# The gate table built 16 tokens at a time: two runs of half-precision matmuls back to back

## The chip, the cores and the metric

The kernel runs on one core of one Trainium2 chip. The metric is the device time of one execution in microseconds (us); lower is better. TensorE multiplies (its rows in the profile are PE for a matmul and PEld for the load of a matmul's weights, the stationary operand), VectorE (DVE) and ScalarE (ACT) do elementwise work, and transfers from memory are issued from the SP queue.

## The reference

One decoder layer on 256 tokens of width 1024: attention and pooling, an output projection, and then the part that matters here, a feed-forward layer (PEER) with 16,384 = 128 x 128 experts of one neuron each. Every token has 8 heads; each head picks 16 experts by two sub-keys of 128 entries, with softmax gates.

```python
def chunk(xc):
    q = jnp.einsum('cd,de->ce', xc, w_q)...reshape(C, PEER_HEADS, 2, half)
    s = jnp.einsum('chpk,pnk->chpn', q, sub_keys)
    sv, si = lax.top_k(s, K)
    ...
    eid = jnp.take_along_axis(cand_id, top_pos, axis=-1)      # 8 x 16 experts of a token
    gate = jax.nn.softmax(top_v, axis=-1)
    act = jax.nn.gelu(jnp.einsum('cd,chkd->chk', xc, expert_u[eid]))
    y = jnp.einsum('chk,chkd->cd', gate * act, expert_v[eid])
```

## The kernel before

The kernel does not gather experts. It computes S = U h for all 16,384 experts and all tokens, applies the gelu to get A, builds a dense gate table W (expert by token, nearly all zeros), and multiplies: G = W * A, then y = G V. There are three stages: a prefix (attention and projections, to about 131 us), phase 1 (the loop at L887: 16 steps of queries, then 128 steps of S, to 566 us) and phase 2 (the loop at L986, y = G V, to the end).

A step of phase 1 handles one tile of 128 rows of weights. `split` (L510) cuts the loaded tile into a high part on ScalarE (L501) and a low part on VectorE (L506), one step ahead of its use; `mm3` (L546) then issues 24 matmuls of 256 columns in a reduced float32 format, 16 from the high part (L551 and L552 in turn) and 8 from the low part (L555). Queries go into PSUM banks 1 to 3, S into banks 6 and 7.

Around these steps the program's order is written by the Python code itself: `after(d, f)` puts a function behind the matmuls of the step d steps later (`run_hooks`), and `run_bg` takes pieces of background work from a list, as many as a budget allows for each step.

The gate table is such background work. For each group of 8 tokens (`c8` from 0 to 31) `wtok` makes four half-precision tiles on VectorE in four pieces: two one-hot tables (`ohb`, `oha`) and `oha` times the high and the low half of the gate (`ah`, `al`). One step later (two for `c8` = 0) `wmm` (L778) issues 16 matmuls of 128 columns, two for each token, into two PSUM banks: 0 and 1 where `c8` is even, 2 and 3 where it is odd. A step after that `wput` (L793) takes the result out of PSUM: multiplied into A by VectorE (L798) where A is there already, copied by ScalarE (L801) elsewhere. `gelu` (L804) treats the tokens whose W is there and those whose W is not there apart; `have["W"]` holds how many there are.

In this text a run is an unbroken row of half-precision matmuls (L782 and L783 in turn), and a stretch is what stands between two runs: one, two or three steps of `mm3`.

Of the kernel before, what the change touches and what calls it, by code (L numbers as in the profile page):

```python
# [18 lines left out]
T = 256  # L19
D = 1024  # L20
# [39 lines left out]
class Loads:  # L60
    """DMAs in the order of their use; each is issued as soon as its pool has a free slot."""

# [25 lines left out]
def _body(ctx, tc, xT, c, w_ada, cols, w_in, pool_w, w_out, peer_wq, subkeys, peer_u, peer_v, final_g,  # L88
# [38 lines left out]

# [1 line left out]
    silc = prep.tile([P, D + 1], F32, name="silc")  # L129
# [51 lines left out]

# [1 line left out]
    nc.vector.memset(ones, 1.0)  # L183
    nc.vector.memset(silc[:, D:D + 1], 1.0)
    # per-head negated score bias of 128 queries and the 256 keys up to the last of them: ALiBi, the window
    # mask and the log of the number of branches; s of the first queries takes the rest of each row
    def score_bias(hs):
# [24 lines left out]
    def rsqrt(r, m, std):  # L212
        """r = 1/sqrt(m), one Newton step on the root of ScalarE."""
        nc.scalar.activation(std, m, AF.Sqrt)
        nc.vector.reciprocal(r, std)
        nc.vector.scalar_tensor_tensor(std, m, -0.5, r, op0=ALU.mult, op1=ALU.mult)
        nc.vector.tensor_mul(std, std, r)
        nc.vector.scalar_tensor_tensor(r, std, 1.5, r, op0=ALU.add, op1=ALU.mult)

    def rstd_rows(ps, psb):  # L220
        """psb[any partition, token] = 1/sqrt(sum/D + eps)."""
        m = prep.tile([P, 6], F32, name="m", bufs=2)
        nc.vector.tensor_scalar(m[:, 0:2], ps, 1.0 / D, EPS, op0=ALU.mult, op1=ALU.add)
        rsqrt(m[:, 2:4], m[:, 0:2], m[:, 4:6])
        dg = prep.tile([P, 2, P], F32, name="dg", bufs=1)
        for tb in range(2):
            nc.vector.tensor_scalar(dg[:, tb, :], ident, m[:, 2 + tb:3 + tb], None, op0=ALU.mult)
        nc.tensor.matmul(psb, lhsT=ones, rhs=dg.rearrange("p a t -> p (a t)"), start=True, stop=True)
# [6 lines left out]
    def keep_warm(n):  # L235
        """matmuls on ones while there is nothing to multiply: TensorE's clock is halved when it is idle"""
        for _ in range(n):
            nc.tensor.matmul(banks[5][:, 0, 0:P], lhsT=ones, rhs=ones, start=True, stop=True)
# [37 lines left out]

# [1 line left out]
    for k in range(KD):  # L278
# [29 lines left out]
        def mm(m, n):  # L308
            """product n (hi hi, hi lo, lo hi) of output block m: 0-7 q k, 8-11 u, 12-13 v"""
            if m < 12:  # L310
                wh, wl = (w0h, w0l) if m < 8 else (w1h, w1l)
                cs = slice(m * P, (m + 1) * P) if m < 8 else slice(512 + (m - 8) * P, 512 + (m - 7) * P)
                a, b = ((wh, hh), (wh, hl), (wl, hh))[n]
                nc.tensor.matmul(banks[m // 2][:, m % 2, :], lhsT=a[:, cs], rhs=b,
                                 start=(st and n == 0 and m % 2 == 0), stop=(sp and n == 2), skip_group_check=True)
            else:
                tb = m - 12
                a, b = ((hh, w1h), (hl, w1h), (hh, w1l))[n]
                nc.tensor.matmul(banks[6 + tb].rearrange("p a t -> p (a t)"), lhsT=a[:, tb * P:(tb + 1) * P],
                                 rhs=b[:, 0:512], start=(st and n == 0), stop=(sp and n == 2))  # L320
# [23 lines left out]

# [1 line left out]
    pra.close()  # L346
# [41 lines left out]
    def s2d(p):  # L388
        for h in (2 * p, 2 * p + 1):
            s = biast[:, h, :]  # L390
            mx = prep.tile([P, 6], F32, name="mx", bufs=4)
            # s = -score, mx = -max score
            for tb, cs, bs in ((0, slice(0, P), slice(256, 384)), (1, slice(P, 384), slice(P, 384))):
                nc.vector.tensor_tensor_reduce(
                    out=s[:, cs], in0=s[:, bs], in1=H[h]["ps"][:, cs], scale=1.0, scalar=-NEG,
                    op0=ALU.add, op1=ALU.min, accum_out=mx[:, tb:tb + 1])
            H[h]["s"], H[h]["mx"] = s, mx
# [92 lines left out]

# [1 line left out]
    x2 = xt  # L492
# [20 lines left out]

    # x2 in token rows, for the last residual
    turned = [banks[i].rearrange("p a t -> p (a t)") for i in (4, 5, 6, 0)]
# [30 lines left out]
    def mm3(o, n, ks=range(KD)):  # L546
        """o[128, T] += (tile n of 8 blocks [d, 128])^T h2"""
        hi, lo = splits[n]
# [8 lines left out]

    # queries: the first two tiles follow the arrival of h2
    # from here on: queries in banks 1 to 3, scores in 4 and 5, S in 6 and 7, W and y in 0 to 3
    def q_bank(n):  # L560
# [35 lines left out]

# [1 line left out]
    NA = 96  # L598
# [31 lines left out]
    def top16(sets):  # L630
        """the 16 largest and their places, for several (vals, idx, src) side by side"""
        lo, hi = slice(0, 8), slice(8, 16)
# [11 lines left out]
    def retrieval(tb):  # L644
# [7 lines left out]
        def second(hh):  # L652
            # pairs (a, b) of the sorted halves: a < 4 with all b, a >= 4 with b < 4; for any other pair
            # 16 pairs of these stand before it
            if hh == 0:
# [15 lines left out]
        def gates():  # L671
            g = S["gate"] = tk.tile([P, NH, TOPK], F32, name="gate")
            nc.vector.tensor_sub(g, S["tv"], S["tv"][:, :, 0:1].to_broadcast([P, NH, TOPK]))
            nc.scalar.activation(g, g, AF.Exp)
            # the places of the first choice, each twice, by half
            S["si2"] = tk.tile([P, 2, NH * TOPK, 2], F16, name="si2")
# [13 lines left out]
        def places():  # L690
            """(a, b) of a place: a = max(pos / 16, pos / 4 - 12), b = pos - min(16 a, 4 a + 48)"""
            sh = [P, NH * TOPK]
# [60 lines left out]

    WS = {}

    def wtok(c8, part):
# [7 lines left out]
        if part == 0:  # L764
            WS["b"] = wp.tile(sh, F16, name="ohb")
            nc.vector.tensor_tensor(out=WS["b"], in0=io, in1=pair(jT), op=ALU.is_equal)
        elif part == 1:
            WS["a"] = wp.tile(sh, F16, name="oha", bufs=1)
            nc.vector.tensor_tensor(out=WS["a"], in0=io, in1=pair(iT), op=ALU.is_equal)
        elif part == 2:  # L770
            WS["h"] = wp.tile(sh, F16, name="ah")
            nc.vector.tensor_tensor(out=WS["h"], in0=WS["a"], in1=pair(gh), op=ALU.mult)
        else:
            WS["l"] = wp.tile(sh, F16, name="al")
            nc.vector.tensor_tensor(out=WS["l"], in0=WS["a"], in1=pair(gl), op=ALU.mult)
            after(1 if c8 else 2, wmm, c8, WS["b"], WS["h"], WS["l"])

# [8 lines left out]
    def parts(lo, hi):  # L786
        """tiles lo..hi of the table, as slices of the two buffers that hold it"""
        for buf, at_, n in ((a0, 0, NA), (P2.get("a1"), NA, NK - NA)):
# [4 lines left out]
    def wput(c8, o):  # L793
        """W of 8 tokens: times A where A is there already, else left in its place"""
        ts = slice(c8 * 8, c8 * 8 + 8)
# [4 lines left out]
        for a, r in parts(have["A"], NK):  # L800
            nc.scalar.activation(a[:, :, ts], oT[:, r, :], AF.Copy, scale=1.0 / GSC)  # L801
        have["W"] = c8 * 8 + 8

    def gelu(i, bank):  # L804
        """A of tiles i, i + 1, times W for the tokens whose W is there"""
        (a, _), = parts(i, i + 2)
# [59 lines left out]

# [1 line left out]
    G = {}  # L868
# [44 lines left out]

# [1 line left out]
    step_no[0] = NQ + NK  # L915
# [62 lines left out]

    # the last tiles serve the first 128 tokens before the others, so that these can be finished early
    spare = [[p3.tile([P, D], F32R, name=x) for x in ("vh", "vl")] for _ in range(2)]  # L980
    spare.append([G[0][j].rearrange("p i t -> p (i t)") for j in (1, 2)])
    # in them, the last quarter of the columns of the other tokens goes to a bank of its own
    pieces = [slice(0, 512), slice(512, 768), slice(768, 1024)]
# [21 lines left out]

# [1 line left out]
    zs = [f3[:, (1 + tb) * D:(2 + tb) * D] for tb in range(2)]  # L1007
# [11 lines left out]
    def z_piece(tb, j, cs, y=None, x=None):  # L1019
        """z = y g2 + x2 and its sum of squares"""  # L1020
        z_add(tb, cs, ycols(tb, cs) if y is None else y, x2nat[:, tb, cs] if x is None else x)
        nc.scalar.activation(sqz[:, cs], zs[tb][:, cs], AF.Square, accum_out=scol(tb, j))
# [11 lines left out]
    def half_inv(tb, j, part):  # L1034
        """1 / (s + m / s): half of 1/sqrt(m), from s near sqrt(m)"""
        if part == 0:
# [98 lines left out]
```

## Time and profile before

| what | value |
|---|---|
| time, median of 3 executions | 928.67 us (928.41 to 928.76) |
| profiled execution, first to last instruction | 930.6 us |
| TensorE busy | 910.1 us, 98% of the span |
| VectorE busy | 691.6 us, 74% |
| ScalarE busy | 455.3 us, 49% |
| half-precision matmuls (L782, L783) | 512, from 306.5 to 540.6 us |

The profiled execution is told by its span alone; it is 1.9 us above the median of the three timed ones. A busy TensorE is one that has a matmul in flight: matmuls overlap, so the record of one (281 ns for 256 columns) is longer than the distance to the next. How fast they follow each other is read from their start times, or from how many of them a stretch holds.

### The profile page before, as it was taken

What the parts mean: (1) busy time and instruction counts of PE and PEld (TensorE: products, weight loads), DVE (VectorE), ACT (ScalarE), POOL (GpSimd) and SP (SyncE); (2) the same over time, 40 slices, a digit from 0 to 9 for tenths busy, and PEclk for the clock granted to TensorE, in tenths of its full rate; (3) what the DMA queues carried; (4) which work ended last, traced back from release to release, by engine and by line L of the source; (5) the groups of instructions that cost most, each with busy time, mean ns of one, the idle gap of its engine ahead of it and who ended that gap; (6) DMA issues with size and microseconds to landing.
All of it is one profiled execution on the core that took longest, in us unless ns stands there. A gap on an engine that the chain in (4) does not pass through costs nothing.

```text
span 930.6 us, 15919 instructions
## 1 busy us (share of the span) xinstructions
PE 910.1 (98%) x6283; PEld 830.6 (89%) x6283; DVE 691.6 (74%) x1285; ACT 455.3 (49%) x655; POOL 10.3 (1%) x19
## 2 busy tenths in 40 slices
PE   7999989999999999999999999999999999999996
PEld 7987889999999999999999998888878788888885
DVE  5999869898989778888888966555556656656665
ACT  3447355545555455454444445444446545444442
POOL 0000000000000000000000000000000000000001
PEclk7999989999999999999999999999999999999999
DMA  9987735455656555555555556666767766667551
GB/s 343 408 312 264 293 107 167 159 182 183 183 190 192 161 164 168 169 161 171 168 160 166 174 167 191 189 195 195 217 217 226 238 226 214 213 210 218 183 180 46
DMA packets 52061, 185.40 MB, mean 199 GB/s; under 512 B 6033, under 2 KB 6545, under 8 KB 51986
## 3 DMA queue, kind: packets, MB, share of 16 engines
q1 hardware_dynamic: 50402, 179.12, 59.4%
q0 software_dynamic: 1440, 5.25, 1.9%
q8 instruction: 49, 0.80, 0.4%
q14 instruction: 26, 0.21, 0.1%
q10 hardware_dynamic: 144, 0.01, 0.0%
HBM read 183.31 MB, written 1.05 MB: 198 GB/s over the span
## 4 chain that ended last, share of the span: by engine, by line
PE 87%; DVE 5%; DMA 4%; ACT 2%; issue 1%; SPq 0%; ACTq 0%; DVEq 0%
PE psum L976 33%; PE psum L551 14%; PE psum L552 14%; PE psum L555 14%; PE psum L441 3%; DMA raw<-in_peer_v_dram 3%; PE psum L782 2%; PE psum L783 2%; PE psum L568 1%; DVE junk L198 1%; DVE wlo L300 1%; PE psum L832 1%; DMA big<-in_w_in_dram 1%; ACT hi L501 1%; DVE lo L506 1%
## 5 line engine op out<-in xcount | busy, mean ns | idle before, releaser
L506 DVE TENSOR_TENSOR lo<-raw,hi 128x1024 fp32r<-128x1024 f32 x269 | 328.6, 1223 | 205.9 <-ACT hi L501 204.9
L501 ACT ACTIVATE hi<-raw 128x1024 fp32r<-128x1024 f32 x269 | 285.0, 1060 | 318.0 <-PE psum L976 153.7
L551 PE MATMUL psum<-h2h,hi 128*128 128x256 f32 x1128 | 273.4, 283 | 0.4 <-ACT q L823 0.4
L552 PE MATMUL psum<-h2l,hi 128*128 128x256 f32 x1128 | 269.7, 280 | 0.0
L551 PEld LDWEIGHTS psum<-h2h,hi 128*128 128x128 f32 x1128 | 213.1, 189 | 0.6 <-ACT q L823 0.6
L552 PEld LDWEIGHTS psum<-h2l,hi 128*128 128x128 f32 x1128 | 213.0, 189 | 0.0
L555 PE MATMUL psum<-h2h,lo 128*128 128x256 f32 x1128 | 154.5, 280 | 0.0
L555 PEld LDWEIGHTS psum<-h2h,lo 128*128 128x128 f32 x1128 | 141.7, 189 | 0.0
L976 PE MATMUL psum<-hi,h2h 128*128 128x512 f32 x486 | 132.8, 393 | 2.3 <-ACT hi L501 2.3
L976 PE MATMUL psum<-lo,h2h 128*128 128x512 f32 x486 | 131.4, 390 | 0.0
L976 PE MATMUL psum<-hi,h2l 128*128 128x512 f32 x486 | 131.3, 390 | 0.0
L976 PEld LDWEIGHTS psum<-hi,h2h 128*128 128x128 f32 x486 | 90.5, 188 | 22.5 <-ACT hi L501 3.5
L976 PEld LDWEIGHTS psum<-lo,h2h 128*128 128x128 f32 x486 | 91.3, 188 | 20.0
L976 PEld LDWEIGHTS psum<-hi,h2l 128*128 128x128 f32 x486 | 91.3, 188 | 19.8
L198 DVE SCALAR_TENSOR_TENSOR junk<-ada,silc 128x1025 f32<-128x1025 f32 x40 | 48.9, 1222 | 0.3
L801 ACT ACTIVATE a<-psum 128x256 f32<-128x256 f32 (+22 forms) x54 | 16.7, 352 | 60.8 <-DVE a L798 52.6
L883 DVE TENSOR_TENSOR h2l<-a,h2h 128x1024 fp32r<-128x1024 f32 x31 | 37.8, 1219 | 0.0
L782 PE MATMUL psum<-ah,ohb 128*128 128x128 f16 x256 | 33.1, 220 | 0.0
L783 PE MATMUL psum<-al,ohb 128*128 128x128 f16 x256 | 32.7, 218 | 0.0
L879 ACT ACTIVATE h2h<-a 128x1024 fp32r<-128x1024 f32 x31 | 32.4, 1045 | 0.0
L441 PE MATMUL psum<-cat,big 128*128 128x256 f32 x128 | 28.9, 382 | 0.0
L441 PEld LDWEIGHTS psum<-cat,big 128*128 128x128 f32 x128 | 23.9, 190 | 3.9 <-issue 0.8
(226 smaller groups left out, 807.9 us busy)
## 6 DMA issues: line engine op xcount, KB each, us to landing
raw<-in_peer_u_dram SPq DMA_DIRECT2D x128, 512.0 KB, 3.6
raw<-in_peer_v_dram SPq DMA_DIRECT2D x128, 512.0 KB, 4.3
ada<-in_w_ada_dram SPq DMA_DIRECT2D x40, 512.5 KB, 7.1
big<-in_w_in_dram SPq DMA_DIRECT2D x16, 512.0 KB, 9.2
raw<-in_peer_wq_dram SPq DMA_DIRECT2D x16, 512.0 KB, 3.7
a<-in_w_ada_dram POOLq DMA_DIRECT2D x8, 512.5 KB, 5.3
big<-in_w_out_dram SPq DMA_DIRECT2D x8, 512.0 KB, 6.5
out_dram<-a SPq DMA_DIRECT2D x4, 256.0 KB, 2.3
```

The source lines that it names most:

```text
L198: nc.vector.scalar_tensor_tensor(jk, blk, 1.0, sil, op0=ALU.mult, op1=ALU.mult, accum_out=ada[:, v * 8 + k:v * 8 + k + 1])
L441: nc.tensor.matmul(ob[m // 2][:, m % 2, :], lhsT=w[:, m * P:(m + 1) * P], rhs=cat[:, k, :], start=(n == 0 and m % 2 == 0), stop=(n == 7), ...
L501: nc.scalar.activation(hi, raw, AF.Copy)
L506: nc.vector.tensor_sub(lo, raw, hi.bitcast(F32))
L551: nc.tensor.matmul(o, lhsT=hi[:, cs], rhs=h2h[:, k, :], start=(k == 0), stop=False, skip_group_check=True)
L552: nc.tensor.matmul(o, lhsT=hi[:, cs], rhs=h2l[:, k, :], start=False, stop=False, skip_group_check=True)
L555: nc.tensor.matmul(o, lhsT=lo[:, cs], rhs=h2h[:, k, :], start=False, stop=(k == KD - 1), skip_group_check=True)
L782: nc.tensor.matmul(o[:, t, :], lhsT=b[:, pr, :, e], rhs=ah[:, pr, :, e], start=True, stop=False)
L783: nc.tensor.matmul(o[:, t, :], lhsT=b[:, pr, :, e], rhs=al[:, pr, :, e], start=False, stop=True)
L879: nc.scalar.activation(hi, a, AF.Copy)
L883: nc.vector.tensor_sub(lo, a, hi.bitcast(F32))
L976: nc.tensor.matmul(ycols(tb, cs) if o is None else o, lhsT=a[:, i % 4, tb * P:(tb + 1) * P], rhs=b[:, cs], start=st, stop=sp, skip_group_c ...
```

## The change

The runs of two neighbouring groups are issued together. `wtok` puts a finished group on a list, and only an odd group asks for the matmuls, one step later; `wmm2` then takes the groups from the end of the list, so that the odd one (banks 2 and 3) goes first and the even one (banks 0 and 1) directly behind it. `al` is written over `oha`, and the tiles have three buffers each. The two `wput` of a pair follow in one step, and `have["W"]` grows by 16.

```diff
+    WP = []
...
         if part == 0:
-            WS["b"] = wp.tile(sh, F16, name="ohb")
+            WS["b"] = wp.tile(sh, F16, name="ohb", bufs=3)
...
-            WS["a"] = wp.tile(sh, F16, name="oha", bufs=1)
+            WS["a"] = wp.tile(sh, F16, name="oha", bufs=3)
...
-            WS["h"] = wp.tile(sh, F16, name="ah")
+            WS["h"] = wp.tile(sh, F16, name="ah", bufs=3)
...
         else:
-            WS["l"] = wp.tile(sh, F16, name="al")
-            nc.vector.tensor_tensor(out=WS["l"], in0=WS["a"], in1=pair(gl), op=ALU.mult)
-            after(1 if c8 else 2, wmm, c8, WS["b"], WS["h"], WS["l"])
+            nc.vector.tensor_tensor(out=WS["a"], in0=WS["a"], in1=pair(gl), op=ALU.mult)
+            WP.append((c8, WS["b"], WS["h"], WS["a"]))
+            if c8 % 2:
+                after(1, wmm2)
+
+    def wmm2():
+
+        while WP:
+            wmm(*WP.pop())
...
-        have["W"] = c8 * 8 + 8
+        have["W"] = max(have["W"], c8 * 8 + 8)
```

On TensorE, the end of the first run before (numbers behind a name are buffers; `ohb` are the weights):

```order
L782 LDWEIGHTS ohb_3451
L782 MATMUL psum_137<-ah_3455,ohb_3451 128x128
L783 LDWEIGHTS ohb_3451
L783 MATMUL psum_137<-al_3499,ohb_3451 128x128
L551 MATMUL psum_137<-h2h_71,hi_3536 128x256
L552 MATMUL psum_137<-h2l_72,hi_3536 128x256
L551 MATMUL psum_137<-h2h_71,hi_3536 128x256
```

And the middle of the first run of the changed kernel (L789 and L790 are the L782 and L783 of before):

```order
L789 LDWEIGHTS ohb_3531
L789 MATMUL psum_137<-ah_3565,ohb_3531 128x128
L790 LDWEIGHTS ohb_3531
L790 MATMUL psum_137<-oha_3533,ohb_3531 128x128
L789 LDWEIGHTS ohb_3451
L789 MATMUL psum_137<-ah_3455,ohb_3451 128x128
L790 LDWEIGHTS ohb_3451
L790 MATMUL psum_137<-oha_3453,ohb_3451 128x128
```

Where a step of `mm3` followed the 16th half-precision matmul, 16 more of the next group follow it, without a wait in between; the run stands where the odd group's stood, behind the same step, and the place of the even group is empty.

On VectorE, the pieces behind the first two groups before:

```order
L775 TENSOR_TENSOR al<-oha,gl 128x1024
L506 TENSOR_TENSOR lo<-raw,hi 128x1024
L798 SCALAR_TENSOR_TENSOR a_1267<-psum,a_1267 128x46x8
L766 TENSOR_TENSOR ohb<-ion,jT 128x1024
L506 TENSOR_TENSOR lo<-raw,hi 128x1024
L798 SCALAR_TENSOR_TENSOR a_1267<-psum,a_1267 128x46x8
L769 TENSOR_TENSOR oha<-ion,iT 128x1024
```

And now:

```order
L775 TENSOR_TENSOR oha<-oha,gl 128x1024
L506 TENSOR_TENSOR lo<-raw,hi 128x1024
L767 TENSOR_TENSOR ohb<-ion,jT 128x1024
L506 TENSOR_TENSOR lo<-raw,hi 128x1024
L805 SCALAR_TENSOR_TENSOR a_1267<-psum,a_1267 128x46x8 x2
L770 TENSOR_TENSOR oha<-ion,iT 128x1024
```

The first of the two results taken out of PSUM has moved behind one more `lo`, to stand beside the second; everything else keeps its order.

## Rows read from the trace of the kernel before

**Rows 1.** The page: busy time of engines, and the granted TensorE clock in 40 slices.

```profile
PE 910.1 (98%) x6283; PEld 830.6 (89%) x6283; DVE 691.6 (74%) x1285; ACT 455.3 (49%) x655; POOL 10.3 (1%) x19
...
PEclk7999989999999999999999999999999999999999
```

**Rows 2.** Stretch of the table: length, busy PE, PEld, DVE, ACT, POOL; clock.

```profile
400.00:450.00 50.00, 50.00 (x480) 49.77 (x480) 42.34 (x56) 24.39 (x45) 0.00 (x0) 1.00 0.51 165
```

**Rows 3.** Timeline around one run: start us, length us, engine, line.

```profile
356.50 0.28 PE L551 MATMUL psum<-h2h,hi 128*128 128x256 f32 x1
356.51 0.19 PEld L552 LDWEIGHTS psum<-h2l,hi 128*128 128x128 f32 x1
356.62 0.28 PE L552 MATMUL psum<-h2l,hi 128*128 128x256 f32 x1
...
357.87 0.23 PE L782 MATMUL psum<-ah,ohb 128*128 128x128 f16 x1
...
357.94 0.22 PE L783 MATMUL psum<-al,ohb 128*128 128x128 f16 x1
...
358.74 0.22 PE L783 MATMUL psum<-al,ohb 128*128 128x128 f16 x1
...
358.77 0.36 PE L551 MATMUL psum<-h2h,hi 128*128 128x256 f32 x1
```

**Rows 4.** Stretches behind even groups: window, length, L552 matmuls (8 a step).

```profile
307.44:310.25 2.81, 1.87 (x8) 1.00 0.67 182
320.62:326.16 5.54, 3.73 (x16) 1.00 0.52 158
...
349.61:357.87 8.26, 5.59 (x24) 1.00 0.55 164
...
sum 102.18, PE 68.99; mean PE 4.31
```

**Rows 5.** Stretches behind odd groups, the same columns.

```profile
311.15:319.72 8.57, 5.79 (x24) 1.00 0.43 130
...
342.97:348.71 5.74, 3.86 (x16) 1.00 0.48 152
...
sum 106.01, PE 71.42; mean PE 4.46
```

**Rows 6.** Stretches of `mm3` away from runs, and the last one behind a run.

```profile
543.54:566.16 22.62, 15.44 (x64) 1.00 0.56 177
187.15:252.16 65.01, 44.37 (x184) 1.00 0.61 187
540.63:543.54 2.91, 1.93 (x8) 1.00 0.67 225
```

**Rows 7.** L552 from 131.5 to 306.5 us: duration in ns, minimum/median/maximum.

```profile
L552 PE MATMUL psum<-h2l,hi x472: 281/281/281, 132.1 to 305.5; 128*128 128x256 f32 x158
```

**Rows 8.** L552 in the stretch from 349.61 us, behind an even group.

```profile
L552 PE MATMUL psum<-h2l,hi x24: 276/276/281, 349.8 to 356.8; 128*128 128x256 f32 x24
```

**Rows 9.** L552 in the stretch from 358.77 us, behind an odd group.

```profile
L552 PE MATMUL psum<-h2l,hi x16: 281/281/281, 359.0 to 363.4; 128*128 128x256 f32 x16
```

**Rows 10.** Waits from 306 to 545 us: total us, times, longest.

```profile
ACT hi L501 <- PE psum L552: 39.0, 25, 1.8
DVE lo L506 <- ACT hi L501: 37.0, 56, 1.5
```

**Rows 11.** VectorE's timeline where its pieces are longest.

```profile
489.12 1.22 DVE L506 TENSOR_TENSOR lo<-raw,hi 128x1024 fp32r<-128x1024 f32 x1
490.26 1.06 DVE L798 SCALAR_TENSOR_TENSOR a<-psum,a 128x768 f32<-128x768 f32 x2
```

**Rows 12.** TensorE's timeline there: the matmuls that read that `lo`.

```profile
494.14 1.07 PE L555 MATMUL psum<-h2h,lo 128*128 128x256 f32 x8
```

**Rows 13.** The chain that ended last, at the start of phase 2.

```profile
566.32 103.49 PE psum L976 x452
```

## Prediction

> **What bounds the kernel now.** I began with the page. TensorE is busy for 98% of the span and its granted clock stands at 9 (0.9 or more) in every slice but two early ones [rows 1]: neither waiting nor the clock's half level can explain much of the time. Next came the windows over the stage in which the table is built: 50.00 us of 50.00 busy, no wait [rows 2]. So the time of this stage is the number of matmuls times the distance from one to the next, and that distance is what I read next.
>
> The timeline around a run shows how a distance comes about [rows 3]. The weights of a matmul begin to load when the matmul ahead starts (356.51 behind 356.50), and the matmul starts 0.11 us after its load began (356.62). Each start is therefore set by the one before, and a shift in time, once there, is handed on. Inside a run the half-precision matmuls follow each other every 0.057 us (14 distances from 357.94 to 358.74).
>
> Then the windows cut at the runs, which show what the page hides: `mm3` has two paces. Behind every even group (banks 0 and 1) two steps take 5.54 us and three take 8.26; behind every odd group (banks 2 and 3) they take 5.74 and 8.57 [rows 4, 5]. The sixteen stretches of either kind hold 37 steps each (8 L552 matmuls make a step): 102.18 us against 106.01. A middle step is 8.26 - 5.54 = 2.72 us or 8.57 - 5.74 = 2.83, that is 113 or 118 ns for each of 24 matmuls. The records say the same without a ruler: an L552 lasts 276 ns at the fast pace and 281 at the slow one [rows 8, 9]. Ahead of the first run all 472 of them last 281 [rows 7], although other work (sub-key scores, transposes) cuts into the steps there too, and behind the last odd run the pace is slow to the end of the stage (8 steps in 22.62 us [rows 6]). TensorE is busy all the same at either pace, with the clock at 1.00, its 2.4 GHz level.
>
> **The change part by part.** It takes away no matmul. It halves the number of runs, doubles their length, and decides which group comes last in each.
>
> *Fewer switches.* The step behind a run takes 2.91 us [rows 6] where an undisturbed one takes 65.01 / 23 = 2.827 [rows 6]: 0.083 lost at each return. Sixteen returns fall away. A run of 16 takes 0.90 us (357.87 to 358.77 [rows 3]); one of 32 should take 0.90 + 16 x 0.057 = 1.81, against 2 x 0.90 = 1.80 for two: 0.014 more. For each pair 0.07 us, in all **-1.1 us**. Bounds: 0, if the longer run pays elsewhere, and -1.3 (16 x 0.083).
>
> *The pace of `mm3` behind the long runs.* This is the large term, and the trace of before does not show it, since no run there has 32 matmuls. In all 32 cases the pace behind a run is fast where the group is even, and in all 32 it is also the opposite of the pace ahead of the run: even groups always came in at the slow pace and odd ones at the fast one [rows 4, 5]. The two readings cannot be told apart by counting:
> - The pace is set by the PSUM banks that the run wrote last. Then every long run, ending in banks 0 and 1, leaves the fast pace.
> - Sixteen half-precision matmuls shift the stream in time, and the shift turns the slow rhythm into the fast one and back. Then 32 of them turn it twice, and the slow pace of the time before the first run stays throughout.
>
> I take the second, for three reasons. Banks as such don't set the pace: the queries' steps write banks 1, 2 and 3, those of S banks 6 and 7, and up to the first run all are slow alike [rows 7]. A finished write to bank 0 has no way to act on a matmul into bank 6 up to three steps and 72 matmuls later, but a shift in time has one, the hand-on of starts [rows 3]. And a run crosses from one bank to the next at its ninth matmul, with no change in its 0.057 us.
>
> With the slow pace throughout, the 37 steps that are fast now cost as much as the 37 slow ones: 106.01 - 102.18 = **+3.8 us**. The bounds of this term are that and the gain if all is fast. The 37 slow steps would save 3.8, less 0.1 because the first stretch (307.44 to 310.25) now comes ahead of the first run; the 8 steps behind the last run save 22.62 - 8 x 2.72 = 0.9 [rows 6, 4]; together -4.6. Phase 2 could keep the fast pace up to where its chain of matmuls first breaks, 452 matmuls on [rows 13]; at 4.5 ns each, as for 256 columns, that is 2.0 more, and 0 if its 512-column matmuls have no second pace.
>
> *VectorE and ScalarE.* The results of two groups come out of PSUM in one step. What is queued behind them is the next `lo`, for which L555 waits. Late in the stage one group's L798 pieces take 1.06 us, so a `lo` may be 1.1 us later than now. It ends at 489.12 + 1.22 = 490.34 and is first read at 494.14: 3.8 us of cover [rows 11, 12]. VectorE waits for `hi` 56 times, and ScalarE for TensorE 25 times [rows 10]; both run ahead. I cost this at nothing; with the cover gone it would be 16 times what exceeds 3.8 us. The third buffer keeps the one-hot tables of a waiting even group, so VectorE need not wait for its matmuls. Writing `al` over `oha` takes the same operation on the same sizes.
>
> The sum: -1.1 + 3.8 = **+2.7 us**. The profiled execution would have 930.6 + 2.7 = 933.3; the median of the runs is 1.9 below its span, so I say **931.4 us** for the median, 0.29% more than before.
>
> [...]
>
> **Rivals.**
> - *All fast, by banks.* -1.1 - 4.6 = -5.7: 923.0 us, and down to 921.0 with phase 2. For it: 32 of 32 stretches fit, and the order odd, even puts banks 0 and 1 last. Against it: the three reasons above. It decides on the first stretch behind the first long run: 2.72 or 2.83 us for a middle step.
> - *Half fast.* The long run as a whole turns the pace once, or which of three buffers holds the tables matters; then about half the steps are fast, as now, and only the switches are saved: 927.5 us. For it: the pace behind 32 matmuls is unmeasured, and the buffers of even and odd groups alternate too. Against it: it asks that 32 matmuls shift the stream just as 16 do.
> - *The long burst makes a `lo` late.* Slower beyond the forecast, from the point where VectorE falls 3.8 us behind; the burst is 1.1. I give it 0.02, within the slower side.
>
> **How the numbers follow.** Slow throughout 0.65 (931.4, its own range 930.4 to 932.4, from the bounds of the switches and 0.2 us between runs of before); half fast 0.13; all fast 0.22, a third of it with a gain in phase 2. A difference under 0.2% (1.9 us) is about what a measurement of this kernel cannot tell from no change. Slower by more: 0.62, all from the first case, whose lower edge can fall under the bound. Within: 0.16. Faster by more: 0.22. Slow and half fast hold 0.78, so the range has to reach the all-fast case: 922.5 to 932.5 us.
>
> **What would show it right or wrong.** Right: the L552 records last 281 ns in all stretches, a middle step takes 2.83 us everywhere, 16 runs take 1.81 us each, and TensorE still waits for nothing in this stage. The pace behind the first long run alone settles the main step. Wrong: 276 ns behind each run (banks), or in every other stretch (a turn by run). If the switches are mis-sized, a run is not 1.81 us, or the step behind it not 2.91. If VectorE matters, L555 waits for `lo` in the list of waits.

## The result, and the profile after

The changed kernel takes 933.98 us (median of 4, 933.76 to 934.11), the kernel before 928.54 beside it: a ratio of 1.0061, 95% interval 1.0040 to 1.0082. That is 5.4 us more, where 2.7 were forecast: the sign holds, the time lies above the range.

The page of the changed kernel looks like that of before [rows 1]; its span is 932.0 us.

```profile
PE 913.3 (98%) x6283; PEld 832.8 (89%) x6283; DVE 693.2 (74%) x1285; ACT 454.9 (49%) x655; POOL 10.4 (1%) x19
...
PEclk7999989999999999999999999999999999999999
```

The same matmuls (x6283) keep TensorE busy 3.2 us longer, with no loss of clock. So the matmuls must follow each other more slowly somewhere, and the windows of L552 say where in phase 1. The first row lies between the two sets of transposes, ahead of the table, and the second between the last transposes and the first long run; then come stretches behind long runs, and the last stretch cut into its first step and the eight others.

```profile
255.14:296.04 40.90, 27.96 (x120) 22.53 (x120) 1.00 0.61 187
296.29:307.68 11.39, 7.72 (x32) 6.06 (x32) 1.00 0.67 207
309.50:323.21 13.71, 9.34 (x40) 7.51 (x40) 1.00 0.50 158
325.03:339.25 14.22, 9.65 (x40) 7.57 (x40) 1.00 0.54 154
...
541.11:544.02 2.91, 1.93 (x8) 1.51 (x8) 1.00 0.60 184
544.02:566.63 22.61, 15.44 (x64) 12.12 (x64) 1.00 0.54 167
```

Five steps (x40) take 13.71 us behind the first run, the fast pace, and 14.22 behind the second. The thirteen runs after that leave 14.22 for five steps or 11.39 for four, and the last one is slow to the end. The step behind a run (2.91) and the eight last ones (22.61) are as before [rows 6]. What nobody asked for is in the first row: 15 steps at the fast pace (40.90 / 15 = 2.727) where no half-precision matmul had run yet. The second transposes turned the stream slow again (four steps in 11.39 us), so the first long run found it slow and left it fast, the second found it fast and left it slow, and only from the third on did a run keep what it found. The records of the two stretches, from 309.50 and from 325.03 us, show the pace as in [rows 8, 9]:

```profile
L552 PE MATMUL psum<-h2l,hi x40: 276/276/285, 309.7 to 322.2; 128*128 128x256 f32 x40
...
L552 PE MATMUL psum<-h2l,hi x40: 281/281/281, 325.2 to 338.2; 128*128 128x256 f32 x40
```

A long run lasts 1.82 us (windows over the first and the second, all of TensorE's matmuls):

```profile
307.68:309.50 1.82, 1.82 (x35) 1.00 0.66 248
323.21:325.03 1.82, 1.82 (x35) 1.00 0.77 257
```

The waits from 306 to 545 us name no wait of TensorE, and ScalarE waits for it more than before (71.8 us, not 39.0 [rows 10]): in this stage the other engines are not late for it.

```profile
ACT hi L501 <- PE psum L552: 71.8, 48, 1.8
DVE lo L506 <- ACT hi L501: 37.3, 55, 1.8
```

From behind the last transposes to phase 2 both kernels have the same 85 steps and 512 half-precision matmuls to do (windows over all of TensorE's matmuls, of before and after). They take 2.15 us more after the change:

```profile
297.97:566.16 268.19, 268.19 (x2556) 1.00 0.54 168
```

```profile
296.29:566.63 270.34, 270.34 (x2555) 1.00 0.54 167
```

The surprise is phase 2. The same 452 matmuls of 512 columns (L983 now) that took 103.49 us [rows 13] take 105.44:

```profile
566.63:672.07 105.44, 105.44 (x452) 85.44 (x453) 1.00 0.63 194
```

That is 105.44 / 452 = 233.3 ns for each instead of 103.49 / 452 = 229.0. It goes on for 684 matmuls, to 726 us, and then the two kernels are alike: 684 x 4.3 ns = 2.9 us. There is a second pace for 512 columns too, and the kernel before had been at the better one.

The two profiles differ by only 932.0 - 930.6 = 1.4 us, since that of before was an unlucky execution: slow between the transposes (42.49 us for the 15 steps), and in phase 2 it waits 2.3 us where the changed kernel waits 0.7. The rows are those of the wait of phase 2 for `hi`, of before and after:

```profile
PE psum L976 <- ACT hi L501: 2.3, 3, 0.9
```

```profile
PE psum L983 <- ACT hi L501: 0.7, 1, 0.7
```

### The profile page after: what moved, and what is told of

Its sections match the earlier page's. It is cut to its first block, busy times and chain, and to the rows that moved or that the text cites. A ratio compares the mean times of both kernels' runs of the same rounds, so it can differ in the third digit from the quotient of the medians.

```text
span 932.0 us, 15904 instructions
## 1 busy us (share of the span) xinstructions
PE 913.3 (98%) x6283; PEld 832.8 (89%) x6283; DVE 693.2 (74%) x1285; ACT 454.9 (49%) x655; POOL 10.4 (1%) x19
## 4 chain that ended last, share of the span: by engine, by line
PE 89%; DVE 5%; DMA 3%; ACT 2%; issue 1%; SPq 0%; ACTq 0%; DVEq 0%
PE psum L983 35%; PE psum L551 14%; PE psum L555 14%; PE psum L552 14%; PE psum L441 3%; PE psum L789 2%; PE psum L790 2%; DMA raw<-in_peer_v_dram 1%; PE psum L568 1%; DVE junk L198 1%; DVE wlo L300 1%; PE psum L839 1%; DMA big<-in_w_in_dram 1%; ACT whi L297 1%; DMA xt<-in_xT_dram 0%
## 5 line engine op out<-in xcount | busy, mean ns | idle before, releaser
L552 PE MATMUL psum<-h2l,hi 128*128 128x256 f32 x1128 | 270.8, 280 | 0.0
L552 PEld LDWEIGHTS psum<-h2l,hi 128*128 128x128 f32 x1128 | 213.3, 189 | 0.0
L983 PE MATMUL psum<-hi,h2h 128*128 128x512 f32 x486 | 133.6, 395 | 0.7 <-ACT hi L501 0.7
L983 PE MATMUL psum<-lo,h2h 128*128 128x512 f32 x486 | 132.5, 393 | 0.0
L983 PE MATMUL psum<-hi,h2l 128*128 128x512 f32 x486 | 132.2, 393 | 0.0
L983 PEld LDWEIGHTS psum<-lo,h2h 128*128 128x128 f32 x486 | 91.5, 188 | 20.7
L983 PEld LDWEIGHTS psum<-hi,h2l 128*128 128x128 f32 x486 | 91.5, 188 | 20.6
L983 PEld LDWEIGHTS psum<-hi,h2h 128*128 128x128 f32 x486 | 90.9, 188 | 20.8 <-ACT hi L501 1.1
L808 ACT ACTIVATE a<-psum 128x256 f32<-128x256 f32 (+15 forms) x54 | 16.0, 349 | 35.9 <-DVE a L805 35.7
L789 PE MATMUL psum<-ah,ohb 128*128 128x128 f16 x256 | 31.2, 219 | 0.0
L790 PE MATMUL psum<-oha,ohb 128*128 128x128 f16 x256 | 31.0, 218 | 0.0
```

The lines of the kernel that those rows point to most:

```text
L552: nc.tensor.matmul(o, lhsT=hi[:, cs], rhs=h2l[:, k, :], start=False, stop=False, skip_group_check=True)
L789: nc.tensor.matmul(o[:, t, :], lhsT=b[:, pr, :, e], rhs=ah[:, pr, :, e], start=True, stop=False)
L790: nc.tensor.matmul(o[:, t, :], lhsT=b[:, pr, :, e], rhs=al[:, pr, :, e], start=False, stop=True)
L983: nc.tensor.matmul(ycols(tb, cs) if o is None else o, lhsT=a[:, i % 4, tb * P:(tb + 1) * P], rhs=b[:, cs], start=st, stop=sp, skip_group_c ...
```

## The experiments

The theory (rhythm): whatever interrupts the stream of `mm3` shifts it in time, and the shift decides the pace behind it, in phase 2 too. The first rival (banks): the PSUM banks written last decide. The second: the buffers, or VectorE's and ScalarE's work beside a run. The times of the kernel before in these runs spread from 925.8 to 934.1 us (64 executions), so that single paces are read from the profiles and only sums from the times.

**The kernel before once more.**

> The kernel before, unchanged, for a second profile. Rhythm (the pace behind an interruption is set by the shift in time that it leaves): in phase 1 again 2.72 us behind every even group and 2.83 behind every odd one, since all distances repeat; the paces of phase 2 or of the steps around the transposes may differ from the first profile, because they hang on when a wait ends. Banks: the same picture in phase 1. If the timed executions (928.5 us) are quicker than the profiled one because of a pace, this profile shows a stretch at 276 ns where the first had 281, or a span nearer to 927.

It took 927.95 us, span 926.2. Windows of L552: between the transposes, behind the first (even) run, behind the second (odd) and third (even), and the last eight steps.

```profile
256.52:297.43 40.91, 27.96 (x120) 22.53 (x120) 1.00 0.57 182
...
310.66:318.91 8.25, 5.59 (x24) 4.51 (x24) 1.00 0.43 136
319.81:325.56 5.75, 3.86 (x16) 3.02 (x16) 1.00 0.44 149
...
543.05:564.71 21.66, 14.90 (x64) 11.92 (x64) 1.00 0.61 186
```

Both theories had expected the first picture again, and both were wrong. The program is the same, and now the odd groups (banks 2 and 3) leave the fast pace (three steps 8.25) and the even ones the slow (two steps 5.75). The transposes had left the stream fast this time, so the first run turned it slow, the second fast, and so on to the end. What stays the same is the turn: 16 half-precision matmuls leave the other pace than they found, here and in each of the 160 runs of 16 in the five profiles that have such runs. That ends the reading by banks.

**The banks exchanged.**

```diff
-        o = psum[:, c8 % 2 * 2:c8 % 2 * 2 + 2, :].rearrange(...)
+        o = psum[:, 2 - c8 % 2 * 2:4 - c8 % 2 * 2, :].rearrange(...)
```

> The kernel before, with even groups in PSUM banks 2 and 3 and odd groups in 0 and 1; nothing else differs. Rhythm: nothing changes, 2.72 us in a middle step behind even groups and 2.83 behind odd ones, 928.5 us. Banks: the two change places, 2.83 behind even groups and 2.72 behind odd ones; that is worth 0.1 us at the first stretch and 0.9 at the last (8 steps), so about 927.5 us. The verdict is the pace behind the first group, not the time.

928.42 us; ratio to before 0.9996 (0.9980 to 1.0013). Odd groups, now in banks 0 and 1, leave the fast pace (second row), even ones the slow (third). By itself that looks like the banks' case; beside the last experiment, which had the same paces with the banks as they were, it is the entry that decides again: the stream came fast to the first run (three steps in 8.27 us ahead of it).

```profile
296.56:304.83 8.27, 5.60 (x24) 4.51 (x24) 1.00 0.70 218
...
309.54:317.80 8.26, 5.59 (x24) 4.51 (x24) 1.00 0.47 139
318.70:324.44 5.74, 3.86 (x16) 3.02 (x16) 1.00 0.44 146
```

**The even group first in each long run.**

```diff
-            wmm(*WP.pop())
+            wmm(*WP.pop(0))
```

> The changed kernel with the even group first in each run, so that banks 2 and 3 are written last. Rhythm: a run of 32 shifts the stream as before; slow (2.83) behind nearly all runs, 934 us. Banks (as far as the changed kernel left them any hold): the pace behind all runs is the same too, but the first, fast one of the changed kernel goes slow.

934.46 us; 1.0057 (1.0036 to 1.0079): the changed kernel's time. Banks 2 and 3 come last now, and the first stretch is fast and the others slow, as in the changed kernel:

```profile
309.16:322.87 13.71, 9.33 (x40) 7.51 (x40) 1.00 0.50 158
324.69:338.91 14.22, 9.65 (x40) 7.57 (x40) 1.00 0.50 152
```

**The buffers alone.** The kernel before with `bufs=3` for `ohb`, `oha`, `ah` and the low part written over `oha`, still 32 single groups.

```diff
-            WS["l"] = wp.tile(sh, F16, name="al")
-            nc.vector.tensor_tensor(out=WS["l"], in0=WS["a"], in1=pair(gl), op=ALU.mult)
-            after(1 if c8 else 2, wmm, c8, WS["b"], WS["h"], WS["l"])
+            nc.vector.tensor_tensor(out=WS["a"], in0=WS["a"], in1=pair(gl), op=ALU.mult)
+            after(1 if c8 else 2, wmm, c8, WS["b"], WS["h"], WS["a"])
```

> The kernel before with only the other half of the change: three buffers for the one-hot tables and the low part written over the table of i, but still one group of 8 tokens at a time (32 runs of 16 matmuls). Rhythm: the pace turns at every run as in the kernel before, 2.72 in one half of the stretches and 2.83 in the other, 928.6 us. If the buffers set the pace or cost VectorE time that TensorE waits for: all stretches alike, or 930 us and more with waits for the low part.

929.58 us; 1.0003 (0.9979 to 1.0027), and the paces take turns (windows of an odd and an even stretch): this half of the change costs nothing.

```profile
344.42:350.16 5.74, 3.86 (x16) 3.02 (x16) 1.00 0.52 163
351.06:359.32 8.26, 5.59 (x24) 4.51 (x24) 1.00 0.54 168
```

**One matmul more in a run.**

```diff
-            wmm(*WP.pop())
+            c8, b, ah, al = WP.pop()
+            wmm(c8, b, ah, al)
+        if c8 > 0:
+            nc.tensor.matmul(psum[:, 5, 0:P], lhsT=b[:, 0, :, 0], rhs=ah[:, 0, :, 0], start=True, stop=True)
```

> The changed kernel with one more half-precision matmul (into bank 5, read by nobody) behind the 32 of every run but the first one: 15 runs of 33. Rhythm: the shift that a run leaves changes by 57 ns, which is not a whole number of the stream's distances, so the pace behind the runs changes in some or all of the 15 stretches; if the first run leaves the fast pace as in the changed kernel, a shift that keeps it gives 2.72 us throughout: 15 runs x 0.06 us dearer, 64 or so steps x 0.11 us cheaper, 928 us. Banks, VectorE or ScalarE as the cause: slow behind all runs as in the changed kernel, 935 us.

925.25 us; 0.9960 (0.9942 to 0.9977): 8.9 us under the median of the changed kernel taken again (934.11, below), for fifteen matmuls more. The first run, of 32, was entered fast and left slow (first row); the second, of 33, turned the stream fast, and every later one kept it so, down to the last eight steps (21.72).

```profile
309.21:323.43 14.22, 9.65 (x40) 7.57 (x40) 1.00 0.47 155
325.31:339.01 13.70, 9.32 (x40) 7.51 (x40) 1.00 0.51 156
340.88:354.58 13.70, 9.31 (x40) 7.51 (x40) 1.00 0.54 159
...
538.02:559.74 21.72, 14.90 (x64) 11.99 (x64) 1.00 0.55 172
```

Of the 81 steps behind the first run 76 are fast where the changed kernel had 5: 71 x 0.107 = 7.6 less, fifteen extra matmuls x 0.057 = 0.9 more. Phase 2 runs at 229 ns too, 2.9 less: 9.6 in sum. My 928 had left out phase 2.

**Runs of 32 to 38.**

```diff
+        for _ in range((0, 1, 2, 1, 3, 1, 4, 1, 5, 1, 6, 1, 1, 0, 1, 1)[c8 // 2]):
+            nc.tensor.matmul(psum[:, 5, 0:P], lhsT=b[:, 0, :, 0], rhs=ah[:, 0, :, 0], start=True, stop=True)
```

> The changed kernel with runs of different lengths: 32, 33, 34, 33, 35, 33, 36, 33, 37, 33, 38, 33, 33, 32, 33, 33 half-precision matmuls (those above 32 go to bank 5 and are read by nobody). Rhythm: the pace behind a run hangs on its length and on the pace ahead. Five half-precision matmuls of 57.3 ns are 286.7 ns, so lengths five apart should do the same: 33 and 38 leave fast when entered fast, 34 to 37 leave slow, 32 (the fourteenth) turns fast to slow. Where 33 is entered slow, fast (as the one case of the runs of 33) or not, which is open. Banks, buffers or a burst of VectorE as the cause: nothing depends on a length.

926.72 us. Windows of L552 behind runs of 33, 34, 35, 33, 36 and 37 in this order (x40 is five steps, x32 four):

```profile
326.37:340.07 13.70, 9.32 (x40) 7.51 (x40) 1.00 0.49 160
342.00:355.71 13.71, 9.33 (x40) 7.51 (x40) 1.00 0.48 157
...
373.28:384.67 11.39, 7.72 (x32) 6.06 (x32) 1.00 0.50 145
386.55:400.77 14.22, 9.65 (x40) 7.58 (x40) 1.00 0.52 153
402.81:416.51 13.70, 9.32 (x40) 7.51 (x40) 1.00 0.51 157
434.19:448.41 14.22, 9.65 (x40) 7.57 (x40) 1.00 0.54 154
```

All sixteen, read so:

| entered | stays or turns fast | leaves slow |
|---|---|---|
| fast | 33 (6 times), 34, 38 | 32, 35, 37 |
| slow | 32 (the first run), 36, 33 (behind 32 and behind 37) | 33 (behind 35) |

The pace hangs on the length, matmul by matmul, and lengths five apart (33 and 38, 32 and 37) agree, as expected; 34 to 38 were seen once each. Three things were not as expected: 34 keeps the fast pace and 36 turns to it, which I had both said would go slow, and 33 entered slow does either. So "slow" does not seem to be one state: what a run makes of it hangs on what had made it slow. The runs of 32 say the same. In all seven profiles that begin with one (the changed kernel twice and five of its variants), the first turned the pace: slow to fast where the stream came in slow, fast to slow where it came in fast. Behind a run of 32 that had left the stream slow, each further one kept it slow.

**Single matmuls, far from any run.**

```diff
+    def extra(count):
+        for _ in range(count):
+            nc.tensor.matmul(psum[:, 5 if "p" in P2 else 0, 0:P], lhsT=ion[:, :, 0], rhs=ion[:, :, 1], start=True, stop=True)
...
+        extra({22: 1, 26: 2, 30: 3, 34: 4, 38: 5}.get(n, 0))
...
+        extra({10: 1, 20: 2, 30: 3, 40: 4}.get(i, 0))
```

> The kernel before with 1, 2, 3, 4 and 5 half-precision matmuls (128 columns of a constant, into bank 0, read by nobody) behind steps 22, 26, 30, 34 and 38, far ahead of the first run, and 1, 2, 3 and 4 of them (bank 5) behind tiles 10, 20, 30 and 40 of phase 2. Rhythm: the pace changes at some of the five places in 187 to 255 us, where all steps now take 2.827 (each turn is visible as 2.72 in the next middle steps, with 276 ns records), and at some of the four in phase 2 the 512-column matmuls go from 228.9 to 233.3 ns or back. If runs need the table's banks, buffers or VectorE's work to change a pace: 2.827 throughout and 228.9 throughout.

931.07 us. The timeline shows the whole interruption, one matmul (L818), and the windows the stretches ahead of it, and behind 1, 4 and 5:

```profile
196.94 0.23 PE L818 MATMUL psum<-ion 128*128 128x128 f16 x1
196.99 0.36 PE L551 MATMUL psum<-h2h,hi 128*128 128x256 f32 x1
```

```profile
182.72:196.94 14.22, 9.65 (x40) 7.58 (x40) 1.00 0.51 170
196.99:207.97 10.98, 7.46 (x32) 6.01 (x32) 1.00 0.59 180
...
230.40:241.39 10.99, 7.47 (x32) 6.01 (x32) 1.00 0.67 194
241.66:255.88 14.22, 9.65 (x40) 7.58 (x40) 1.00 0.59 184
```

One matmul that holds the next start back by 0.05 us turned the stream from slow to fast; 2, 3 and 4 kept it fast; 5 turned it back. All fifteen go to bank 0, so the bank doesn't make the difference between one to four and five, and the tables, their buffers and the work on them come only later. In phase 2, which was at 229 ns, none of the four extras changed the pace.

**The last run alone.** In the changed kernel only the last run gets its 33rd matmul.

```diff
+        if c8 == 30:
+            nc.tensor.matmul(psum[:, 5, 0:P], lhsT=b[:, 0, :, 0], rhs=ah[:, 0, :, 0], start=True, stop=True)
```

> The changed kernel with one more half-precision matmul (bank 5, read by nobody) behind the last of its 16 runs alone: it isolates the end of phase 1 and the pace of phase 2. Rhythm: slow up to the last run as in the changed kernel; behind it the 8 or 9 last steps at 2.72 instead of 2.83 (0.9 us less), and phase 2, entered from another rhythm, starts with 512-column matmuls of 228.9 ns instead of 233.3 (684 of them, 3.0 us less): 934.2 - 3.9 = 930.3 us. If the slow 512-column matmuls come from something else (DMA, the table's place, the state of the buffers): 0.9 less at most, 933.3 us.

In the profile both parts came: the last eight steps are fast (windows of L552, ahead of the last run and behind it), and phase 2 starts at 103.45 / 452 = 228.9 ns (window of L986).

```profile
531.68:543.08 11.40, 7.72 (x32) 6.06 (x32) 1.00 0.48 147
...
547.81:569.53 21.72, 14.90 (x64) 11.97 (x64) 1.00 0.54 172
```

```profile
569.53:672.98 103.45, 103.45 (x452) 84.89 (x453) 1.00 0.66 198
```

The median is 932.49 us, 1.0035 (1.0012 to 1.0058): 1.6 us under the changed kernel's 934.11, not 3.9. The executions spread over 929.66 to 935.77. Grouped, once the times were known, by the mean granted clock over the span, the four at 0.988 or more have a median of 930.35, against 933.98 for eight such ones of the changed kernel (with the even group first or not): 3.6 less. Among the others the gap is only 0.7 (933.6 to 934.25). So the paces are shown; their full worth in the median is not.

**Extras in phase 2 alone.** The changed kernel, with the `extra` of above behind tiles 4, 8, 12 and 16 of phase 2.

```diff
+        extra({4: 1, 8: 2, 12: 3, 16: 4}.get(i, 0))
```

> The changed kernel with 1, 2, 3 and 4 half-precision matmuls (bank 5, read by nobody) behind tiles 4, 8, 12 and 16 of phase 2; nothing else differs. Rhythm: phase 2 starts at 233.3 ns, and at one of the four the 512-column matmuls turn to 228.9 ns and stay there, which saves 4.4 ns on each of the 500 to 640 that were slow still, 2.2 to 2.8 us less 0.5 for the extras: 932 us. If the slow 512-column matmuls come from DMA or the buffers: 233.3 on to the first wait, 934.5 us.

933.25 us; 1.0048 (1.0033 to 1.0063). Windows of L987 ahead of the first extra and between the first and the second:

```profile
569.68:583.72 14.04, 14.04 (x61) 11.19 (x61) 1.00 0.62 187
584.04:594.57 10.53, 10.53 (x47) 8.64 (x46) 1.00 0.63 190
```

The first window holds 60 distances and the extra itself (0.04 us): 14.00 / 60 = 233.3 ns. The second holds 46: 10.53 / 46 = 228.9. One half-precision matmul ended the slow pace of 512 columns, and it stayed ended. The expected time was 932. The nine executions lie at 930.96 to 935.05, and their median is 0.9 us under the changed kernel's 934.11, so here too the pace is shown and its full worth in the median is not.

**The changed kernel once more.**

> The changed kernel, unchanged, for a second profile and more times beside the others. Rhythm: slow (2.83) behind all runs but perhaps the first, 233.3 ns at the start of phase 2, 934 us; the steps around the transposes may be at either pace. If 233.3 ns at the start of phase 2 was a thing of the one execution: 228.9 here.

934.11 us; 1.0058 (1.0036 to 1.0079). Now the first transposes left slow, the second fast (windows of L552), the first run came in fast and left slow, and so did all others. Phase 2 is at 105.47 / 452 = 233.3 ns again (window of L983, whose count takes in the matmul at its end).

```profile
256.75:299.24 42.49, 28.94 (x120) 22.72 (x120) 1.00 0.57 185
299.48:310.47 10.99, 7.46 (x32) 6.01 (x32) 1.00 0.63 195
312.29:326.51 14.22, 9.65 (x40) 7.57 (x40) 1.00 0.55 154
```

```profile
569.93:675.40 105.47, 105.47 (x453) 85.44 (x453) 1.00 0.61 194
```

**33 everywhere, and one matmul at 190 us.** `if c8 > 0` goes, and `extra({20: 1}.get(n, 0))` comes behind step 20.

> The changed kernel with 33 half-precision matmuls in all 16 runs, and one single half-precision matmul (bank 0, read by nobody) behind step 20, at about 190 us, where the single one turned the pace before. Rhythm: 2.72 from there to the transposes (22 or 23 steps by 0.107 us, 2.4 us less), and 2.72 behind all or nearly all runs and to the end: about 925.2 - 2.4 = 922.8 us. If the single matmul's turn does not last or is given back where a transfer then ends last: 925 us.

923.90 us (922.30 without the two executions above 930); 0.9958 (0.9927 to 0.9990), a profiled execution of 919.70. All is fast from 190 us to the end of phase 1 (windows: the 23 steps that took 65.01 before [rows 6], and the last nine):

```profile
189.67:252.33 62.66, 42.85 (x184) 34.54 (x184) 1.00 0.60 191
...
532.03:556.60 24.57, 16.76 (x72) 13.52 (x72) 1.00 0.57 180
```

Its ten executions spread more than any other's (919.70 to 934.82); what the two above 930 had in them no trace shows.

**One more behind each group of scores.** The same with `extra(1)` at the end of `q_scores`.

> The same, with one more half-precision matmul behind each of the eight groups of sub-key score matmuls, which stand between the steps of 131 to 187 us. Rhythm: if the single matmul turns the pace there as it does behind step 20, up to 17 steps by 0.107 less, 1.8 us, for eight by 0.05 dearer: 921.4 us. If the stream that it finds behind the score matmuls is at another point of the rhythm: 2.83 as before there and 0.4 us dearer, 923.2 us.

922.43 us; 0.9929 (0.9901 to 0.9957), not told apart from the kernel before it in this list (922.30). Up to the matmul behind step 20 the records stay at the slow 281 ns, so a single matmul does not turn the pace where score matmuls stand ahead of it.

```profile
L552 PE MATMUL psum<-h2l,hi x119: 281/281/281, 144.8 to 191.8; 128*128 128x256 f32 x119
```

## Why the prediction was right in sign and wrong in size

- **Fewer switches, -1.1.** Held: runs of 1.82 us (forecast 1.81), 2.91 behind them. With the next term it makes +2.2; the windows from the last transposes to phase 2 show 270.34 - 268.19 = +2.15.
- **The pace behind the long runs, +3.8.** The size held but for the first stretch, whose five steps turned fast: 3.8 - 5 x 0.107 = +3.3. The mechanism held only in part. That 16 turn the stream, whatever the bank, is shown (the kernel before once more). That 32 turn it twice, and so keep the pace they find, is not so: the first long run turned it in every profile that begins with one of 32, slow to fast here (11.39 us for four steps ahead of it, 13.71 for five behind), fast to slow when the changed kernel ran once more, and 33 keep it fast where 32 do not. The slow stream of the forecast came because 32 make a fast stream slow and keep the slow one that they make, which I had not foreseen: that the size is so near is in part luck.
- **Phase 2, bounded by 0 and -2.0 and taken as 0: the step that failed, and that put the time outside the range.** I wrote that phase 2 could gain 2.0 if its 512-column matmuls had a second pace, and nothing if not. They have one, and before was at the better: +2.9, shown by the windows of two executions (105.44 and 105.47) and ended by one matmul. The trace of before gave no row of a slower pace there, but [rows 13] gave no reason that 229 was the slow one either. The bound needed both signs. The pace of `mm3` at the end of phase 1 does not foretell that of phase 2: phase 1 ended slow in the profile of before [rows 6] as in the changed kernel's, and phase 2 ran at 229 ns there and at 233.3 here. What a run of 32 hands on to phase 2 stays open.
- The sum is then -1.1 + 3.3 + 2.9 = +5.1, against 5.4 measured. Not in it are the pace between the transposes, which differs from one execution to the next by 1.6 us, and what a second pace does to the waits for loads in phase 2 (2.3 us in one profile of before, none in the other).
- **The range of the slow case, 930.4 to 932.4.** It does not come out of its own terms: switches worth between 0 and -1.3 beside +3.8 give 931.2 to 932.5 us, and with the 0.2 us between runs the upper end lies over the 932.5 of the whole range. The 0.2 us stood on three executions; 64 of the kernel before spread over 8.3 us.
- **Every L552 ahead of the first run is slow, although other work cuts in [rows 7].** True of that execution, but not a rule: the first transposes left the stream fast in the profile of the changed kernel and in the second one of the kernel before. I had read one draw as a rule, and with it the tie of even groups to the fast pace.
- **VectorE and ScalarE, 0.** Held: no wait of TensorE in the table's stage, and the buffers alone are 1.0003.
- **All fast, by banks** fell with the kernel before once more; its prize was there all the same, for one matmul more. **Half fast** did not come, though the first long run turned the pace once, as it asks. The **late `lo`** did not come.

The Trainium skill (TensorE: Matmul & The Clock Gate, section Back-to-back issue gap) has two figures for 512 columns: columns / 2.4 plus 2.5 ns for an isolated warm matmul, by estimate 216 ns, and about 131 ns in a sustained stream of weight loads and matmuls. The windows of this stream show neither figure: they have 228.9 and 233.3 ns at a granted clock of 1.00, two distances where the page has one for a stream.

## What to carry to other kernels

Where TensorE is never idle and the clock is full, divide windows between interruptions by the number of matmuls: if equal work has two paces, a reordering can move the time by turning the pace, and a single cheap matmul at the right place may be worth more than the reordering. Look at two or three executions before calling a pattern a rule, and where a pace has not been seen, bound it on both sides. Here 33 matmuls instead of 32 in all runs but the first made the change worth 0.4% instead of costing 0.6%.

## What the runs showed of the hardware that I had not expected

- A stream of 256-column matmuls holds 2.720 or 2.827 us for 24 of them until something interrupts it; one matmul of 128 half-precision columns, 0.05 us, turned it (five steps in 14.22 us ahead of it, four in 10.98 behind).
- 512-column matmuls have two paces too, 228.9 and 233.3 ns, and hold one for 684 matmuls.
- The same program takes different paces in different executions: 15 steps between its transposes took 40.91 or 42.49 us.
- What in TensorE makes two rhythms of one stream the profile doesn't show: the records of a weight load are alike at both (187/188/191 and 187/188/192 ns). That an interruption acts by its shift in time is argued, not shown, for no run holds the number of matmuls and changes the time alone. The number by itself does not decide: the same three transposes left the same kernel's stream slow in one execution and fast in another (42.49 and 40.91 us above), and 32 matmuls do either with a stream that they find slow. That stays open.
